# An eleventh 2 MB place for expert weights from the start, the first value projection in one stream of both weight parts, and the last tokens turned before a gather

## The chip, the cores and the metric

The kernel runs on one core of one Trainium2 chip. Its time is the device time of one execution in microseconds (us). The engines are TensorE (PE in the profile; PEld is its weight loading), VectorE (DVE), ScalarE (ACT), GpSimd (POOL) and SyncE (SP, which here only issues DMA). Each engine works through its own instructions in the order in which the program wrote them; semaphores order the engines among each other.

## The reference

One decoder layer for 256 tokens of width 1024, all in float32:

```python
proj = h @ w_in[layer]                       # 1024 -> 4360 columns
qa, ka, va, qf, kf, vf, fl, ga, gf = jnp.split(proj, split_points, axis=-1)
ya = sliding_window_sink_attention(qa, ka, va, sink) @ w_proj_swa     # 8 heads, 2 key/value heads, window 128
yf = forgetting_attention(qf, kf, vf, log_sigmoid(fl + b_forget)) @ w_proj_fox   # 8 heads
mix = sigmoid(ga) * ya + sigmoid(gf) * yf
h = layer_norm(ALPHA * h + mix @ w_out)
m = moe(h)        # softmax router, top 4 of 32 experts, clamped SwiGLU, 1024 -> 2 x 1024 -> 1024
h = layer_norm(ALPHA * h + m)
```

The 32 experts hold 8 MB of gate and up weights and 4 MB of down weights each, 384 MB in all, and every one is read once.

## The kernel before

**Two phases.** The front (to about 200 us) does the input projection, both attentions, the gated mix, the output projection, the first layer norm and the routing. Then come 32 experts, each on 64 gathered token rows, two experts to a gather (`OH`, `OH0` are the one-hot matrices; `xTe` holds the gathered rows).

**Precision in the front.** A projection is made of three passes, high by high, high by low and low by high part. `split` (L108) makes the parts of a weight group: ScalarE copies the high part (L110), VectorE subtracts it to get the low part (L111). `projT` (L312 to L314) gives transposed results, `projN` (L325 to L327) results with tokens on the partitions. The weight groups of `w_in` arrive one after the other by DMA (L218) and are split by `split_in`; `evac` copies a finished PSUM tile, alternating between ScalarE (L93) and VectorE (L95, L97). PSUM tiles of projections are named `pj` and have two buffers. Group 0 is the keys of the windowed attention, group 1 its values together with the 8 forget-gate columns (128 + 8 = 136 columns), groups 2 and 3 its queries. The order in the program is

```python
split_in(0); split_in(1); split_in(2)
projT(0, ka)
split_in(3)
projN(1, [(v[:, :, 0:128], 0, 128), (fl, 128, 136)])     # both token halves in one tile pj
...
for i in range(2, 8): split_in(i + 2); projT(i, ...)
```

**Mix and output projection.** 32 pieces of `w_proj_swa`, `w_proj_fox` and `w_out` (128 x 512 each, numbered u) are split by `split_u`, most of them into the tile `w_r` with five buffers; some go into other tiles (u = 5 to 8 and the even ones from 24). The loop at L569 uses the pieces in the order 0 to 12, 14, 13, 15, twelve matmuls each (L576 to L578), and after most of them writes a split some pieces ahead. The last pieces end in the gate products and sums on VectorE (L584, L585), the mix's high and low halves (L586 on ScalarE, L566 on VectorE) and the output projection (`out_proj`, L614).

**Layer norm and routing.** `residual`, `shift`, `normed`, `turn` (transposes at L644 and their copy), `logits` (L658), `choice`, `positions` (L675) and `gather0` (L684) run for token half 0 and then for half 1. `busy` (L102) issues filler matmuls. `scaled_out` (L824, L822) writes the gathered rows of experts 0 and 1.

**Weights of the experts.** The first 32 items of 2 MB (four of gate and up, two of down per expert) go into ten places of 16 KB per partition (`slot_tile`), which the front uses for its own data, and one further place, `extra`. `load_next` issues the next item on SyncE (L127), `refill` does so as the experts use items up. In the front, places are filled as they come free: two at the first pair of heads, then behind pieces 7, 15, 15, 15, 23, 31, then two in the routing and last `extra`, when the pool `p2` of the front is closed. `extra` is used once, for item 10. From item 32 on, the memory of the ten places becomes five places of 4 MB (`ww`), each loaded with two items in one transfer.

Of the kernel before, what the change touches and what calls it, by code (L numbers as in the profile page):

```python
# [35 lines left out]
def layer(tc, x, w_in, b_forget, sink, w_proj_swa, w_proj_fox, w_out, ln1_g, ln1_b, w_router, b_router,  # L36
# [9 lines left out]
    with ExitStack() as ctx:  # L46
# [5 lines left out]
        slots = {i: small.enter_context(tc.tile_pool(name=f"slot{i}", bufs=1, side="right")) for i in reversed(slot_of[1:] + slot_of[:1])}  # L52
# [19 lines left out]
        alpha_i = per.tile([P, P], F32, name="alpha_i")  # L72
# [69 lines left out]
        def load_next(n=1):  # L142
            for _ in range(n):
                i = nxt[0]
                kind, e, q = items[i]
                if i < SMALL:
                    r = extra.tile([P, 4096], F32, name="w") if i == 10 else slot_tile(slot_of[(i - (i > 10)) % 10])
                    where[kind, e, q] = r
                    fetch(kind, slice(e, e + 1), q, r)
                    nxt[0] += 1  # L150
                    continue
                r = big_tile()
                where[kind, e] = r
                for a in range(2):
                    where[kind, e, q + a] = r[:, 4096 * a:4096 * a + 4096]
                if i + 2 < len(items):
                    fetch(kind, slice(e, e + 1), q, r, 2, 4 if i + 8 >= len(items) else 2 if i + 26 >= len(items) else 1)
                else:
                    fetch_last(r)
                nxt[0] += 2  # L160

        def refill(n, keep=0):

            used[0] += n
            while nxt[0] < len(items):
                i = nxt[0] + (nxt[0] >= SMALL)
                if i - (11 if i < 21 else 10) >= used[0] - keep:
                    break
                if nxt[0] >= SMALL and not big:
                    if used[0] < SMALL:  # L170
                        break

                    extra_ctx.close()
                    small.close()
                    for u in reversed(range(5)):
                        big.append(ctx.enter_context(tc.tile_pool(name=f"two{u}", bufs=1, side="right")))
                    big.reverse()
                load_next()
# [18 lines left out]
        with tc.tile_pool(name="hd", bufs=1) as hd:  # L197
# [25 lines left out]
            with ExitStack() as at_ctx:  # L223
# [12 lines left out]
                dve.tensor_scalar(alpha_i, ident, ALPHA, None, op0=OP.mult)  # L236
# [45 lines left out]
                def split_in(i, parts=(0, 1)):  # L282
# [3 lines left out]
                    if i not in hls:  # L286
                        tl = slot_tile(1 + i % 3, F32R)
                        hls[i] = [tl[:, 8 * n * k:8 * n * (k + 1)].rearrange("p (c n) -> p c n", n=n) for k in (0, 1)]
                    for q in parts:
                        cs = slice(4 * q, 4 * q + 4)  # L290
                        for k, r in enumerate(raws[i]):
# [5 lines left out]
                            else:  # L297
                                split(*[a[:, cs, 128 * k:128 * k + m] for a in hls[i]], r[:, cs])
# [46 lines left out]
                projN(1, [(v[:, :, 0:128], 0, 128), (fl, 128, 136)])  # L345
# [128 lines left out]
                def split_u(u):  # L474
# [7 lines left out]
                    elif u > 23 and u % 2 == 0:  # L482
                        if u == 24:
                            more2.append(slot_tile(9, F32R))
                        w_r = more2[0][:, 512 * (u - 24):512 * (u - 22)].rearrange("p (k n) -> p k n", k=2)
                    else:
                        w_r = p2.tile([P, 2, 512], F32R, name="w_r", bufs=5)
# [5 lines left out]
                for i in range(10):  # L493
# [12 lines left out]
                    if i == 0:  # L506
# [13 lines left out]
                        load_next(2)  # L520
                    if i == 7:
# [33 lines left out]
            wb = hd.tile([P, 8, NE], F32, name="wb")  # L555
            gnat = hd.tile([P, 2, 8], F32, name="gnat")
            sums = hd.tile([P, 2, NE], F32, name="sums")
# [41 lines left out]
            mv = hd.tile([P, 2, 2], F32, name="mv")  # L599
            stt = [hd.tile([P, 2, 6], F32, name=f"stt{t}") for t in range(2)]  # L600
            rs = hd.tile([P, 2], F32, name="rs")
            nm = hd.tile([P, 2], F32, name="nm")
            OH0 = hd.tile([P, 2, 2, CAP], F32, name="OH0")
            tix = hd.tile([P, 2, 8], mybir.dt.uint32, name="tix")
            iota_e = hd.tile([P, NE], F32, name="iota_e")
            lgN = hd.tile([P, 2, NE], F32, name="lgN")
            shf = hd.tile([P, 2, NE], F32, name="shf")
# [8 lines left out]
            def residual(t, k):  # L616
# [4 lines left out]
                if k:  # L621
                    dve.bn_aggr(mv[:, t], stt[t])
                    act.activation(rs[:, t:t + 1], mv[:, t, 1:2], AF.Sqrt, bias=eps)

            def shift(t):
                dve.reciprocal(rs[:, t:t + 1], rs[:, t:t + 1])
# [42 lines left out]
            def positions(t, pause=None):  # L669
# [3 lines left out]
                if pause:  # L673
                    pause(3)
# [37 lines left out]
            for c in (4, 5):  # L712
                out_proj(c, 1, 0)
            turn(0, 0, act)
            turn(0, 1, act)
            shift(0)
# [17 lines left out]
            gather0(0, 0)  # L734
            turn(1, 1, act)
            shift(1)
            logits(1, 1)
# [5 lines left out]
            busy(idle, 2)  # L743
# [6 lines left out]
            extra_ctx = ExitStack()  # L750
            extra = extra_ctx.enter_context(tc.tile_pool(name="extra", bufs=1, side="right"))
            load_next()

        with tc.tile_pool(name="mo", bufs=1) as mo:
# [193 lines left out]

            xTs[0] = mo.tile([P, 8, 2, CAP], F32, name="xTe", bufs=2)
# [16 lines left out]
            for e in range(NE):  # L966
# [18 lines left out]
                if e == REST:  # L985
# [5 lines left out]
                    act.activation(gateT, pt[:NE], AF.Copy)  # L991
                    for t in range(2):
# [128 lines left out]
```

## Time and profile before

| | |
|---|---|
| median of 3 runs | 1119.88 us (1118.96 to 1120.91) |
| profiled execution | 1119.41 us |
| its span | 1117.2 us |
| TensorE busy | 1054.9 us (94%) |
| VectorE, ScalarE busy | 378.3 us, 211.3 us |
| mean granted TensorE clock | 0.985 |
| read from memory | 430.53 MB |

The span is the time between the first and the last instruction in the profile; the execution's own time has 2.2 us more. Matmuls are pipelined, so the busy time of TensorE counts overlapping instructions once and is not a measure of full speed. A clock of 1.00 is 2.4 GHz, 0.50 is 1.2 GHz.

### The profile page before, as it was taken

Reading aid. Unit: us, or ns where it says so; the run is one execution under the profiler, and the core shown is the slowest. Engines: PE = TensorE matmul, PEld = TensorE weight load, DVE = VectorE, ACT = ScalarE, POOL = GpSimd, SP = SyncE. Lnnn points to the kernel's source line nnn. Section 1 sums busy time; section 2 is a strip of 40 time slices with the busy share of each in tenths; the row PEclk is TensorE's granted clock in tenths of the full one; section 3 lists DMA queues with packets and bytes.
Section 4 is the critical chain, followed back from the end, with each engine's and each line's share of the span. In section 5 each row is a group of like instructions: output and inputs, shape, how many; then the busy total and the mean of one; then the engine's idle time right before and its main releaser. Section 6 shows DMA issues by size and latency. Waiting matters only on the chain. (4 is left out here: it accounts for less than half of the span.)

```text
span 1117.2 us, 13432 instructions
## 1 busy us (share of the span) xinstructions
PE 1054.9 (94%) x5677; PEld 517.1 (46%) x5677; DVE 378.3 (34%) x821; ACT 211.3 (19%) x416; POOL 4.8 (0%) x14
## 2 busy tenths in 40 slices
PE   9999999999999999999999999999998988998895
PEld 8988897533333333333333343333433333333322
DVE  5577476432222224222222222222222222222223
ACT  5466464311111110000000110011000000000011
POOL 0000000000000000000000000000000000000001
PEclk9999999999999998999999999999999999999997
DMA  9754599999999999999999999999999999999993
GB/s 274 227 195 146 140 392 354 377 426 405 429 424 429 432 431 416 430 429 430 430 430 431 429 432 431 431 431 430 429 429 431 430 429 430 426 425 428 423 419 121
DMA packets 46406, 432.48 MB, mean 387 GB/s; under 512 B 5524, under 2 KB 26020, under 8 KB 29448
## 3 DMA queue, kind: packets, MB, share of 16 engines
q1 hardware_dynamic: 46144, 431.18, 93.5%
q8 instruction: 46, 0.75, 0.3%
q10 hardware_dynamic: 200, 0.41, 0.1%
q14 instruction: 16, 0.13, 0.0%
HBM read 430.53 MB, written 1.05 MB: 386 GB/s over the span
## 5 line engine op out<-in xcount | busy, mean ns | idle before, releaser
L851 PE MATMUL G<-ww,xTe 128*64 128x512 f32 x1664 | 368.2, 597 | 19.5 <-DMA ww<-in_w_gate_up_dram 19.1
L851 PEld LDWEIGHTS G<-ww,xTe 128*64 128x64 f32 x1664 | 119.3, 138 | 264.1 <-issue 227.3
L886 PE MATMUL X<-ww,aT 128*64 128x512 f32 x864 | 191.3, 595 | 0.5 <-DVE tb L871 0.3
L858 DVE COPY G_sb<-G 128x512 f32<-128x512 f32 x32 | 33.2, 1037 | 408.0 <-PE G L851 408.0
L860 ACT ACTIVATE G_sb<-G 128x512 f32<-128x512 f32 x32 | 33.8, 1055 | 422.3 <-PE G L851 422.3
L886 PEld LDWEIGHTS X<-ww,aT 128*64 128x64 f32 x864 | 59.6, 137 | 113.4 <-issue 107.6
L851 PE MATMUL G<-w,xTe 128*64 128x512 f32 x384 | 83.5, 593 | 0.6 <-POOL nth L773 0.6
L312 PE MATMUL pj<-w 128*128 128x256 f32 x232 | 66.7, 288 | 1.3 <-ACT w L110 0.8
L314 PE MATMUL pj<-w 128*128 128x256 f32 x232 | 65.7, 283 | 0.2 <-DVE w L111 0.2
L313 PE MATMUL pj<-w 128*128 128x256 f32 x232 | 65.6, 283 | 0.0
L809 PE MATMUL X<-OH,h_perm 128*128 128x128 f32 x480 | 63.0, 288 | 1.2 <-DVE h_perm L947 0.9
L900 PE MATMUL acc<-D_sb,GT 64*128 64x512 f32 x248 | 61.6, 615 | 0.7 <-DVE D_sb L893 0.7
L809 PEld LDWEIGHTS X<-OH,h_perm 128*128 128x128 f32 x480 | 60.1, 204 | 1.8 <-PE X L839 1.2
L868 PE MATMUL X<-ident,G_sb 128*128 128x128 f32 x256 | 40.0, 280 | 20.1 <-ACT xTe L822 12.0
L873 ACT ACTIVATE sg<-tb 128x256 f32<-128x256 f32 x64 | 26.7, 416 | 148.5 <-DVE tb L872 148.5
L851 PEld LDWEIGHTS G<-w,xTe 128*64 128x64 f32 x384 | 28.3, 137 | 53.6 <-issue 52.3
L893 DVE COPY D_sb<-X 128x256 f32<-128x256 f32 x31 | 13.2, 425 | 112.0 <-ACT D_sb L892 112.0
L111 DVE TENSOR_TENSOR w<-w 128x1024 fp32r<-128x1024 f32 (+2 forms) x50 | 46.3, 965 | 13.8 <-ACT w L110 13.8
L312 PEld LDWEIGHTS pj<-w 128*128 128x128 f32 x232 | 44.3, 191 | 3.9 <-issue 2.2
L871 DVE TENSOR_TENSOR tb<-X,bT 128x512 f32<-128x512 f32 x64 | 43.7, 683 | 4.1 <-PE X L868 4.1
L314 PEld LDWEIGHTS pj<-w 128*128 128x128 f32 x232 | 44.4, 191 | 0.4 <-DVE w L111 0.4
L313 PEld LDWEIGHTS pj<-w 128*128 128x128 f32 x232 | 44.4, 191 | 0.0
(263 smaller groups left out, 866.6 us busy)
## 6 DMA issues: line engine op xcount, KB each, us to landing
ww<-in_w_gate_up_dram SPq DMA_DIRECT2D x44, 4096.0 KB, 27.2
ww<-in_w_down_dram SPq DMA_DIRECT2D x23, 4096.0 KB, 28.2
w<-in_w_gate_up_dram SPq DMA_DIRECT2D x24, 2048.0 KB, 10.0
ww<-in_w_gate_up_dram SPq DMA_DIRECT2D x12, 2048.0 KB, 38.5
w<-in_w_down_dram SPq DMA_DIRECT2D x8, 2048.0 KB, 10.7
w<-in_w_in_dram SPq DMA_DIRECT2D x14, 1024.0 KB, 5.6
ww<-in_w_down_dram SPq DMA_DIRECT2D x6, 2048.0 KB, 39.7
ww<-in_w_gate_up_dram SPq DMA_DIRECT2D x8, 1024.0 KB, 28.3
```

The lines of the kernel that those rows point to most:

```text
L111: dve.tensor_tensor(lo, src, hi.bitcast(F32), op=OP.subtract)
L312: pe.matmul(pt[:, j, :], hi[:, c, cs], xh[:, c, :], start=c == 0, stop=False)
L313: pe.matmul(pt[:, j, :], hi[:, c, cs], xl[:, c, :], start=False, stop=False)
L314: pe.matmul(pt[:, j, :], lo[:, c, cs], xh[:, c, :], start=False, stop=c == 7)
L809: pe.matmul(pt[:, c, :], h_perm[:, t, c0 + c, :], OH[:, t].rearrange("p a s -> p (a s)"), start=t == 0, stop=t == 1)
L851: pe.matmul(G[hf][64 * k:64 * k + 64, :], xT_e[:, c, :], w[:, c % 2, n0:n0 + 512], start=c == 0, stop=c == 7)
L858: dve.tensor_copy(dst, src)
L860: act.activation(dst, src, AF.Copy)
L868: pe.transpose(pt[:, c].rearrange("p k s -> p (k s)"), G_sb[:, c0 + c, :], ident)
L871: dve.tensor_tensor(tb, pt, bias[:, c0:c0 + 4, :, None].to_broadcast([P, 4, 2, CAP]), op=OP.add)
L886: pe.matmul(pt[64 * k:64 * k + 64, :], aT[:, c, :], w[:, c % 4, k * 512:(k + 1) * 512], start=c == 0, stop=c == 7)
L900: pe.matmul(acc[t][k], GT[r, t * P:(t + 1) * P], D_sb[r, :], start=first, stop=False)
```

## The change

`extra` is open from the beginning and takes its place as the third of a ring of eleven; item 2 is loaded into it in the attention (pair 3), and every later load of the front is one item further. The ring of eleven holds for all 32 small items. `w_r` has four buffers instead of five, `alpha_i` is made at expert 14, and the small tiles of the layer norm and the routing (`wb`, `gnat`, `sums`, `mv`, `stt`, `rs`, `nm`, `OH0`, `tix`, `iota_e`, `lgN`, `shf`) move from the pool `hd`, which is open all through the front, to `p2`, which opens after the attention. The order of the small places in memory is turned by one. The first gathered rows take the second buffer of `xTe`.

The first values (group 1) lay their high and low parts side by side, so that one matmul of 272 columns gives high by high and high by low; each token half has a PSUM tile of its own, and the two parts are added on the way out.

In the layer norm the square root moves from `residual` to `shift`; for the first half `shift` is written ahead of the two turns, for the second half the turn and `shift` come ahead of the first gather. The filler matmuls between the second half's choice and its positions go from 2 + 3 to 1 + 1.

```diff
-        slots = {i: ... for i in reversed(slot_of[1:] + slot_of[:1])}
+        slots = {i: ... for i in reversed(slot_of[9:] + slot_of[:9])}
+        extra = extra_ctx.enter_context(tc.tile_pool(name="extra", bufs=1, side="right"))
+        ring = [*slot_of[:2], None, *slot_of[2:]]
...
-                    r = extra.tile([P, 4096], F32, name="w") if i == 10 else slot_tile(slot_of[(i - (i > 10)) % 10])
+                    r = extra.tile([P, 4096], F32, name="w", tag="w") if i % 11 == 2 else slot_tile(ring[i % 11])
...
-                if i - (11 if i < 21 else 10) >= used[0] - keep:
+                if i - (11 if nxt[0] < SMALL else 10) >= used[0] - keep:
...
+                        if i == 1:
+                            both = tl[:, :16 * n].rearrange("p (c k n) -> p c k n", k=2, n=n)
+                            hls[i] = [both[:, :, 0], both[:, :, 1], both]
...
-                projN(1, [(v[:, :, 0:128], 0, 128), (fl, 128, 136)])
+                for t in range(2):
+                    pt = pjp.tile([P, 2, 136], F32, name="pj")
+                    ts = slice(t * P, (t + 1) * P)
+                    for c in range(8):
+                        w = hls[1][2][:, c].rearrange("p k n -> p (k n)")
+                        pe.matmul(pt.rearrange("p k n -> p (k n)"), xh[:, c, ts], w, start=c == 0, stop=False)
+                        pe.matmul(pt[:, 0], xl[:, c, ts], hls[1][0][:, c, :], start=False, stop=c == 7)
+                    vl = at.tile([P, 136], F32, name="vl")
+                    act.activation(vl, pt[:, 1], AF.Copy)
+                    dve.tensor_tensor(v[:, t, 0:128], pt[:, 0, :128], vl[:, :128], op=OP.add)
+                    dve.tensor_tensor(fl[:, t], pt[:, 0, 128:], vl[:, 128:], op=OP.add)
...
-                        w_r = p2.tile([P, 2, 512], F32R, name="w_r", bufs=5)
+                        w_r = p2.tile([P, 2, 512], F32R, name="w_r", bufs=4)
...
+                    if i == 3:
+                        load_next()
...
-                    act.activation(rs[:, t:t + 1], mv[:, t, 1:2], AF.Sqrt, bias=eps)
...
             def shift(t):
+                act.activation(rs[:, t:t + 1], mv[:, t, 1:2], AF.Sqrt, bias=eps)
...
-                    pause(3)
+                    pause(1)
...
+            shift(0)
             turn(0, 0, act)
             turn(0, 1, act)
-            shift(0)
...
             residual(1, 1)
-            gather0(0, 0)
             turn(1, 1, act)
             shift(1)
+            gather0(0, 0)
             logits(1, 1)
...
-            busy(idle, 2)
+            busy(idle, 1)
...
-            extra_ctx = ExitStack()
-            extra = extra_ctx.enter_context(tc.tile_pool(name="extra", bufs=1, side="right"))
-            load_next()
...
+            mo.tile([P, 8, 2, CAP], F32, name="xTe", bufs=2)
             xTs[0] = mo.tile([P, 8, 2, CAP], F32, name="xTe", bufs=2)
...
+                    alpha_i = mo.tile([P, P], F32, name="sg", bufs=2)
+                    dve.tensor_scalar(alpha_i, ident, ALPHA, None, op0=OP.mult)
```

## Rows read from the trace of the kernel before

**Rows 1.** The page: span, moved GB/s in 40 slices, one costly group

```profile
span 1117.2 us, 13432 instructions
...
GB/s 274 227 195 146 140 392 354 377 426 405 429 424 429 432 431 416 430 429 430 430 430 431 429 432 431 431 431 430 429 429 431 430 429 430 426 425 428 423 419 121
...
L851 PE MATMUL G<-ww,xTe 128*64 128x512 f32 x1664 | 368.2, 597 | 19.5 <-DMA ww<-in_w_gate_up_dram 19.1
```

**Rows 2.** Stretches: length, busy (instructions) of PE, PEld, DVE, ACT, POOL, clock, DMA, GB/s

```profile
100.00:125.00 25.00, 25.00 (x209) 22.29 (x208) 18.84 (x44) 16.11 (x40) 0.00 (x0) 1.00 0.27 86
200.00:205.00 5.00, 4.62 (x22) 1.96 (x24) 2.71 (x11) 3.24 (x9) 0.45 (x3) 1.00 0.58 242
...
225.00:400.00 175.00, 166.02 (x840) 66.88 (x837) 45.13 (x102) 22.87 (x44) 0.00 (x0) 1.00 1.00 425
```

**Rows 3.** Timeline of SyncE: two single loads (start, length, line, transfer)

```profile
204.07 0.33 SPq L127 DMA_DIRECT2D w<-in_w_gate_up_dram  x1
...
327.37 0.33 SPq L127 DMA_DIRECT2D ww<-in_w_gate_up_dram  x1
```

**Rows 4.** Timeline of TensorE, 12 to 30 us, first matmuls of four projections

```profile
12.16 0.23 PE L325 MATMUL pj<-w 128*128 128x136 f32 x1
...
17.48 0.33 PE L312 MATMUL pj<-w 128*128 128x256 f32 x1
...
23.32 0.39 PE L312 MATMUL pj<-w 128*128 128x256 f32 x1
...
29.80 0.36 PE L312 MATMUL pj<-w 128*128 128x256 f32 x1 [0.47 <-DVE w L97]
```

**Rows 5.** Timeline of ScalarE and VectorE, 15 to 24 us

```profile
16.09 0.36 ACT L93 ACTIVATE w<-pj 128x256 f32<-128x256 f32 x1
...
20.15 1.67 ACT L110 ACTIVATE w<-w 128x512 fp32r<-128x512 f32 x3 [1.74 <-DMA w<-in_w_in_dram]
...
20.81 1.90 DVE L111 TENSOR_TENSOR w<-w 128x512 fp32r<-128x512 f32 x3 [1.68 <-ACT w L110]
22.63 0.42 DVE L95 COPY v<-pj 128x256 f32<-128x256 f32 x1
```

**Rows 6.** TensorE's three longest waits for DMA; one stretch with its clock

```profile
842.38 8.55 PE L851 MATMUL G<-ww,xTe 128*64 128x512 f32 x32 [2.52 <-DMA ww<-in_w_gate_up_dram]
...
901.34 7.09 PE L851 MATMUL G<-ww,xTe 128*64 128x512 f32 x32 [3.26 <-DMA ww<-in_w_gate_up_dram]
...
930.91 8.66 PE L851 MATMUL G<-ww,xTe 128*64 128x512 f32 x32 [3.04 <-DMA ww<-in_w_gate_up_dram]
...
842.00:844.00 2.00, 1.62 (x4) 0.53 (x6) 0.00 (x0) 0.00 (x0) 0.00 (x0) 0.50 0.99 426
```

**Rows 7.** Timeline, 158 to 164 us: first gate product, output projection

```profile
158.02 0.68 DVE L584 TENSOR_TENSOR w<-w,G 128x512 f32<-128x512 f32 x1
...
160.75 3.25 PE L614 MATMUL acc<-w_r,w 128*128 128x512 f32 x12
```

**Rows 8.** Timeline, 191 to 215 us: routing of half 1 and first expert

```profile
191.19 1.14 PE L684 MATMUL X<-OH,h_perm 128*128 128x128 f32 x8
...
192.17 0.60 PE L644 MATMUL G<-ident,x_sb 128*128 128x128 f32 x4
...
193.52 1.08 PE L658 MATMUL acc<-wr,hT 128*128 128x32 f32 x8 [0.75 <-ACT hT L647]
...
195.77 0.38 DVE L667 TENSOR_REDUCE mask<-sel 128x32 f32<-128x128 f32 x1
...
196.74 0.31 PE L675 MATMUL acc<-mask,tri 128*128 128x32 f32 x2
...
197.75 2.02 PE L684 MATMUL X<-OH,h_perm 128*128 128x128 f32 x16 [0.17 <-DVE OH L679]
...
199.87 0.41 DVE L824 TENSOR_SCALAR xTe<-X,gcol 128x128 f32<-128x128 f32 x1 [2.27 <-PE X L684]
...
200.38 13.95 PE L851 MATMUL G<-w,xTe 128*64 128x512 f32 x64 [0.61 <-POOL nth L773]
```

More of the change, by code (lines that the diff above doesn't have):

```diff
@@ L51, in layer @@
         small = ExitStack()
-        slots = {i: small.enter_context(tc.tile_pool(name=f"slot{i}", bufs=1, side="right")) for i in reversed(slot_of[1:] + slot_of[:1])}
+        slots = {i: small.enter_context(tc.tile_pool(name=f"slot{i}", bufs=1, side="right")) for i in reversed(slot_of[9:] + slot_of[:9])}
+        extra_ctx = ExitStack()
+        extra = extra_ctx.enter_context(tc.tile_pool(name="extra", bufs=1, side="right"))
+        ring = [*slot_of[:2], None, *slot_of[2:]]
         ctx.enter_context(tc.manual_schedule())
@@ L71, in layer @@
         warm = per.tile([P, 1], F32, name="warm")
-        alpha_i = per.tile([P, P], F32, name="alpha_i")
         top = per.tile([P, 2, 8], F32, name="top")
@@ L235, in layer @@
                 dve.tensor_scalar(ident, jp, 0.0, None, op0=OP.is_equal)
-                dve.tensor_scalar(alpha_i, ident, ALPHA, None, op0=OP.mult)
                 pool.iota(iota_s, pattern=[[1, CAP]], base=1, channel_multiplier=0,
@@ L297, in split_in @@
                             else:
-                                split(*[a[:, cs, 128 * k:128 * k + m] for a in hls[i]], r[:, cs])
+                                split(*[a[:, cs, 128 * k:128 * k + m] for a in hls[i][:2]], r[:, cs])
                     if 1 in parts and i != 11:
@@ L552, in acc_tiles @@
                 return [[accp.tile([P, 512], F32, name=f"acc{t}{k}") for k in range(2)] for t in range(2)]
-            wb = hd.tile([P, 8, NE], F32, name="wb")
-            gnat = hd.tile([P, 2, 8], F32, name="gnat")
-            sums = hd.tile([P, 2, NE], F32, name="sums")
+            wb = p2.tile([P, 8, NE], F32, name="wb")
+            gnat = p2.tile([P, 2, 8], F32, name="gnat")
+            sums = p2.tile([P, 2, NE], F32, name="sums")
             lower = acc_tiles()
@@ L598, in layer @@
             r = x_sb
[L599 to L607, printed above, removed]
+            mv = p2.tile([P, 2, 2], F32, name="mv")
+            stt = [p2.tile([P, 2, 6], F32, name=f"stt{t}") for t in range(2)]
+            rs = p2.tile([P, 2], F32, name="rs")
+            nm = p2.tile([P, 2], F32, name="nm")
+            OH0 = p2.tile([P, 2, 2, CAP], F32, name="OH0")
+            tix = p2.tile([P, 2, 8], mybir.dt.uint32, name="tix")
+            iota_e = p2.tile([P, NE], F32, name="iota_e")
+            lgN = p2.tile([P, 2, NE], F32, name="lgN")
+            shf = p2.tile([P, 2, NE], F32, name="shf")
             pool.iota(iota_e, pattern=[[1, NE]], base=0, channel_multiplier=0, allow_small_or_imprecise_dtypes=True)
```

## The prediction

> **What bounds the kernel now.** I read the page first, then the busy time by stretch, then the queue of the loading engine, then the waits of TensorE. The page puts 19.1 us of TensorE's waiting at the gate and up matrices on DMA [rows 1]: late in the kernel the weights, not the matmuls, set the pace. The page's slices of 28 us say how evenly: from the ninth to the last but one they carry 405 to 432 GB/s [rows 1]. The stretches say since when: DMA is full from 225 us on, and in 200 to 205 us it was only 58% busy [rows 2]. The end is therefore "the moment the weight stream gets going" plus a fixed number of bytes plus the tail. What gets it going is TensorE: the first refill is issued at 204.07 [rows 3], when the first expert, started at 200.38 [rows 8], has used its first 2 MB place; 16 of its matmuls take half of 7.09 us [rows 6], so 203.9. All eleven places were full by then, which is what the idle DMA share says. So one microsecond in the start of the experts is one microsecond at the end, and the 200 us in front of it are a TensorE matter: from 100 to 125 us TensorE counts 25.00 of 25 us busy beside a DMA share of 0.27 [rows 2].
>
> **The eleventh place.** It moves one 2 MB load from the end of the front into the attention (behind the third pair of heads' projection). At 430 GB/s 2.1 MB are 4.9 us of DMA. It is put into a stretch where DMA is 27% busy [rows 2], and SyncE queues behind it only a 1 MB load whose data are needed two projections later: cost nothing; with that cover gone, at most the 4.9 us. Gain: before and after, eleven items are resident when the first place comes free, so the stream starts no earlier by it. What remains is that eleven, not ten, places turn over among the first 32 items. The average of 225 to 400 us lies at 425 GB/s [rows 2] against 430 in most later slices [rows 1], so at most 175 x 5/430 = 2.0 us can be won there. But at 327.37 the queue again waits for TensorE to free a pair of places [rows 3], the same pair in both versions, and by then the DMA has nearly caught up: I take 0, bounds 0 and -2.0.
>
> **First values in one stream.** Before, 48 matmuls of 136 columns run from 12.16 to 17.48, 0.111 us each; the 256-column ones that follow need 5.84/48 = 0.122 us [rows 4]. So 136 columns cost hardly less than 256, and replacing three passes of 136 by one of 272 (0.122 x 272/256 = 0.129) and one of 136 saves, for 16 pairs, 5.32 - 16 x 0.240 = 1.5 us of TensorE. The Trainium skill (TensorE: Matmul & The Clock Gate, Back-to-back issue gap) gives an isolated matmul columns/2.4 GHz + 2.5 ns, which would make three passes of 136 178 ns and the new two 175 ns, so that by it even this 1.5 us would be nothing; the row's 111 ns stands here.
>
> But the two token halves now take two PSUM tiles of "pj", which has two buffers, where both halves shared one. Follow them. The first half takes the buffer that is free and runs from 12.16 to 14.1. The second needs the buffer of the key projection, whose copy sits on ScalarE behind the splits of the third weight group and runs at 16.09 for 0.36 us [rows 5]: second half from 16.5 to 18.4. The next projection needs the first half's buffer, so its ScalarE copy and its two VectorE additions. In program order these stand behind the splits of the fourth weight group, which wait for that group's data: ScalarE is through at 20.15 + 1.67 = 21.82, VectorE at 20.81 + 1.90 = 22.71 [rows 5]. The values' copy of before started just there, at 22.63, and took 0.42 us for 128x256 [rows 5]; the additions of one half are 128x128 and 128x8, about as long together. So the projection that began at 17.48 begins at about 23.15. Before, this lateness was hidden: the copy's buffer was wanted only at 23.32 [rows 4]. From there two projections of 5.8 us each run to 34.7, against 29.80 before (which holds 0.47 us of waiting, covered now [rows 4]). The later projections keep TensorE at 25.00 of 25 us [rows 2], so nothing gives it back: **+4.9 us** (4.6 to 5.2).
>
> TensorE stands idle for 2.4 us and then for 4.7 us. Three long waits of before bear on its clock: after 2.52 and 3.04 us the granted clock was 0.50 (1.2 instead of 2.4 GHz) and the next 32 matmuls took 8.55 and 8.66 us; after 3.26 us they took 7.09 [rows 6]. The gap here is longer than all three, so I take the loss, 8.6 - 7.09 = **+1.5 us**; bounds 0 and 1.6 (one fall). The Trainium skill (the same page, HAM oscillation) lets every such wait for data cost the clock; the 3.26 us row disagrees once in three, so by the page the 1.5 us are certain, and by the rows likely.
>
> **Four instead of five split buffers.** Each split writes a buffer that its earlier user must have read. With four, the split of piece 17 (ScalarE, then VectorE), written ahead of the first products with the sigmoid gate, waits for a piece among 13 to 16 to be used; before, piece 12 sufficed. A piece is 12 matmuls, 1.4 us; the last ends where the output projection starts, 160.75 [rows 7], so the last but two (piece 14) ends at 157.95 and the last but one (piece 13) at 159.35. After 0.6 us of ScalarE and 0.65 of VectorE (thirds of the rows of three splits [rows 5]) VectorE is at 159.3 or 160.7 with what began at 158.02 [rows 7]. Queued behind it are the gate products, the mix's high halves and the output projection that waits for them: +1.3 us if the buffer that comes free first is taken, +2.7 if they go round in turn. VectorE has no pause in that chain. I take **+1.3**; for the low end 0.5, part of it hidden.
>
> **Last tokens turned first.** The four transposes (192.17) go ahead of the gather (191.19, about 1 us), and the square root behind their copy. The gather then fills the copy's time, and the second logits, at 193.52 after 0.75 us of waiting, start at 191.3 + 0.6 + 1.0 = 192.95 [rows 8]: 0.55 earlier. The choice's mask, ready at 195.77 + 0.38 = 196.15, moves with it, and the position matmul, held until 196.74 by filler matmuls, of which three go, follows the mask at once: 1.0 earlier [rows 8]. The gathered rows were scaled at 199.87, only after all 16 matmuls of 2.02 us, and the experts began at 200.38, 0.61 us after the gather [rows 8]. The scaling's target and the one-hot now lie apart, so the first half is scaled under the second: 0.6 more. **-1.6** (bounds -0.9, if that wait stays, and -1.7). The multiples of the identity made later, the moved small tiles and the square root of the first half sit beside running matmuls: 0; the DVE work at the middle expert is less than 1 us at a place where TensorE's wait for DMA has not begun, so uncovered it would cost under 1.
>
> **The sum.** 4.9 + 1.5 + 1.3 - 1.6 + 0 = +6.1. The profiled execution took 1119.41 us, 2.2 of them outside its span of 1117.2 [rows 1]; it would take 1125.5. The median lies 0.47 higher: **1126.0 us**, 0.55% slower. Own range from the bounds: 4.6 + 0 + 0.5 - 1.7 - 2.0 = +1.4 to 5.2 + 1.6 + 2.7 - 0.9 = +8.6, that is 1121.3 to 1128.5.
>
> **Rivals.** (1) The copies of the first half are not held up, or the next projection gets another buffer. Then the joined stream ends at 16.0, the two projections follow with small waits for the fourth group (VectorE through at 22.71) and the place of 29.80 is reached some 1.4 us sooner. In all -1.4 + 1.3 - 1.6 = -1.7: 1118.2 us, no change or a little faster. It decides if those copies run before 17.5. For it: ScalarE and VectorE do stand idle about 18 to 20 us. Against it: the copy of before had the same idle time in front of it, with its matmuls done at 17.6, and ran at 22.63 [rows 5]. By the skill's spacing its -1.4 would be about 0 and its time 1119.6. Chance 0.13.
> (2) The end is set by bytes alone: with the eleventh place filled early the stream runs through the start of the experts, and their start does not matter. Then one place's 4.9 us are won: 1115.0 us. For it: the full DMA from 225 us on [rows 2]. Against it: the 58% in 200 to 205 us and the refill issued at 204.07, right on TensorE's first place [rows 2, 3]. Chance 0.09.
> My forecast has 0.78, and within it the variants without the fall of the clock (1124.5) or with buffers in turn (1127.4).
>
> **Numbers.** About 0.2% (2.2 us) is what a measurement of this kernel can tell from no change: faster below 1117.6, slower above 1122.1. The forecast lies slower with 0.74 and the same with 0.04; rival 1 the same with 0.08 and faster with 0.05; rival 2 faster with 0.07 and the same with 0.02. Faster 0.12, same 0.14, slower 0.74. The range 1118.5 to 1129.0 takes in the forecast's own range and half of rival 1 and leaves out rival 2.
>
> **What would show it.** Right: TensorE idle from about 18.4 to 23.1 us with VectorE's first addition near 22.7; the granted clock at 0.5 just behind; the first expert near 206.5, the first refill 3.6 us after it; DMA engines idle some microseconds before that; from there the same pace. Wrong: a next projection near 16 to 18 us (rival 1); a first expert that is late while the last weights land early (rival 2); the output projection following its last piece without a pause (no cost of four buffers); scaled rows still waiting for all 16 gather matmuls (tail -0.9 only). If the experts start late and the end is not late, my link from start to end is wrong.

## The result and the profile after

| | before | after |
|---|---|---|
| median of 5 runs | 1119.88 us | 1126.80 us (1124.71 to 1128.36) |
| profiled execution, its span | 1119.41, 1117.2 us | 1127.54, 1125.6 us |
| first expert starts | 200.38 | 208.61 |
| from there to the end of the span | 916.8 | 917.0 |
| mean granted TensorE clock | 0.985 | 0.978 |

The ratio of the runs is 1.0059, with a 95% interval of 1.0043 to 1.0074: 0.6% slower, 6.9 us, where 6.1 us were forecast. The table says where to look: the 8.2 us of the trace are all there when the experts start. The profiled executions lie further apart (8.1 us) than the medians: that of the kernel after took 0.7 us more than its median, that of before 0.5 less.

The page of the kernel after (span, moved GB/s by slice, two costly groups), as in [rows 1]:

```profile
span 1125.6 us, 13394 instructions
...
GB/s 272 178 222 206 103 340 369 297 427 427 427 425 431 428 431 420 429 431 429 428 433 432 430 430 429 431 429 428 434 429 432 429 428 429 426 427 427 422 418 105
...
L865 PE MATMUL G<-ww,xTe 128*64 128x512 f32 x1664 | 370.7, 601 | 17.0 <-DMA ww<-in_w_gate_up_dram 16.6
...
L316 PE MATMUL pj<-w 128*128 128x256 f32 x232 | 67.6, 291 | 2.5 <-DVE fl L360 1.9
```

Late in the kernel the picture is that of before: 429 GB/s or so, TensorE waiting for weights. New is the last line: projections that wait for the forget gates' addition.

The timeline of the kernel after, 12 to 28 us, answering to [rows 4, 5] (start, length, engine and line, idle time ahead and what ended it):

```profile
12.49 0.29 PE L355 MATMUL pj<-w 128*128 128x272 f32 x1
...
16.91 0.36 ACT L95 ACTIVATE w<-pj 128x256 f32<-128x256 f32 x1
...
17.32 0.59 PE L355 MATMUL pj<-w 128*128 128x272 f32 x1 [2.82 <-ACT w L95]
...
20.08 1.67 ACT L112 ACTIVATE w<-w 128x512 fp32r<-128x512 f32 x3 [1.08 <-DMA w<-in_w_in_dram]
20.75 1.90 DVE L113 TENSOR_TENSOR w<-w 128x512 fp32r<-128x512 f32 x3 [1.02 <-ACT w L112]
...
22.56 0.28 DVE L359 TENSOR_TENSOR v<-pj,vl 128x128 f32<-128x128 f32 x1
22.76 0.15 DVE L360 TENSOR_TENSOR fl<-pj,vl 128x8 f32<-128x8 f32 x1
...
23.06 0.55 PE L316 MATMUL pj<-w 128*128 128x256 f32 x1 [1.95 <-DVE fl L360]
...
27.46 0.28 PE L318 MATMUL pj<-w 128*128 128x256 f32 x1
```

The reader is to see a queue, not a slow instruction. The second token half (17.32) waits for the key copy; the next projection (23.06) waits for the first half's additions, and these stand on VectorE behind splits that wait for the fourth group's data. The stretches of the same time (length, busy and instructions of PE, PEld, DVE, ACT, POOL, clock, DMA, GB/s) show the clock:

```profile
18.00:20.00 2.00, 2.00 (x11) 2.00 (x11) 0.69 (x1) 0.63 (x1) 0.00 (x0) 0.50 1.13 331
...
24.00:26.00 2.00, 2.00 (x12) 2.00 (x11) 1.15 (x7) 1.81 (x4) 0.00 (x0) 0.50 0.99 293
...
28.00:30.00 2.00, 2.00 (x19) 2.00 (x19) 1.81 (x2) 0.00 (x0) 0.00 (x0) 1.00 0.06 19
```

At 0.50 only 11 or 12 matmuls go into 2 us, at 1.00 it is 19. The clock had fallen already behind the first wait, so that the second half itself ran slowly, and was back at about 27.4.

The timeline further on, answering to [rows 7, 8] (first mix matmul; split of piece 17 and first gate product; output projection; last gather, scaling, first expert):

```profile
145.15 0.39 PE L593 MATMUL acc<-w,w_r 128*128 128x256 f32 x1 [1.14 <-ACT w_r L112]
...
166.22 0.63 ACT L112 ACTIVATE w_r<-w 128x512 fp32r<-128x512 f32 x1 [0.94 <-PE G L595]
...
167.49 0.68 DVE L601 TENSOR_TENSOR w<-w,G 128x512 f32<-128x512 f32 x1
...
169.61 0.73 PE L631 MATMUL acc<-w_r,w 128*128 128x512 f32 x2 [0.56 <-ACT w L603]
...
170.88 2.60 PE L631 MATMUL acc<-w_r,w 128*128 128x512 f32 x10 [0.53 <-DVE w L583]
...
205.95 2.05 PE L701 MATMUL X<-OH,h_perm 128*128 128x128 f32 x16 [0.27 <-ACT h_perm L651]
...
208.10 0.41 DVE L838 TENSOR_SCALAR xTe<-X,gcol 128x128 f32<-128x128 f32 x1 [2.39 <-PE X L701]
...
208.61 6.66 PE L865 MATMUL G<-w,xTe 128*64 128x512 f32 x30 [0.61 <-POOL nth L787]
```

The split at 166.22 waits for TensorE, with the gate product behind it; the output projection now has pauses (0.56, 0.53) where it had none [rows 7]. The scaling at 208.10 still begins after all 16 gather matmuls. And 145.15 shows what the prediction did not have: 1.14 us of waiting for a split of `w_proj_swa`. The same line of before, with the one where the third dozen of output matmuls begins (177.21 in the kernel after):

```profile
137.59 0.39 PE L576 MATMUL acc<-w,w_r 128*128 128x256 f32 x1 [0.23 <-ACT w_r L110]
...
167.75 0.50 PE L614 MATMUL acc<-w_r,w 128*128 128x512 f32 x1 [0.59 <-ACT w_r L110]
```

The stretch around the start of the experts, in the kernel after (columns as above, DMA share and GB/s last):

```profile
205.00:215.00 10.00, 9.12 (x52) 5.00 (x53) 5.03 (x18) 4.48 (x11) 0.46 (x3) 1.00 0.30 103
```

DMA is busy for 30% of these 10 us; from 208 to 212 it moves 4 GB/s. The first refill is issued at 212.30, 3.7 us after the first expert started, which is the distance of before (204.07 and 200.38 [rows 3, 8]).

### The profile page after: what moved, and what is told of

Same layout as the page of the kernel before. It is cut to its first block, busy times and chain, and to the rows that moved or that the text cites. A ratio compares the mean times of both kernels' runs of the same rounds, so it can differ in the third digit from the quotient of the medians.

```text
span 1125.6 us, 13394 instructions
## 1 busy us (share of the span) xinstructions
PE 1060.5 (94%) x5655; PEld 520.9 (46%) x5655; DVE 379.3 (34%) x824; ACT 212.3 (19%) x417; POOL 4.8 (0%) x14
## 5 line engine op out<-in xcount | busy, mean ns | idle before, releaser
L316 PE MATMUL pj<-w 128*128 128x256 f32 x232 | 67.6, 291 | 2.5 <-DVE fl L360 1.9
L318 PE MATMUL pj<-w 128*128 128x256 f32 x232 | 66.5, 287 | 0.2 <-DVE w L113 0.2
L317 PE MATMUL pj<-w 128*128 128x256 f32 x232 | 66.5, 287 | 0.0
L316 PEld LDWEIGHTS pj<-w 128*128 128x128 f32 x232 | 45.3, 195 | 5.0 <-issue 4.3
L318 PEld LDWEIGHTS pj<-w 128*128 128x128 f32 x232 | 45.4, 196 | 0.4 <-DVE w L113 0.4
L317 PEld LDWEIGHTS pj<-w 128*128 128x128 f32 x232 | 45.4, 196 | 0.0
## 6 DMA issues: line engine op xcount, KB each, us to landing
ww<-in_w_down_dram SPq DMA_DIRECT2D x23, 4096.0 KB, 27.4
```

Source lines behind the costliest of these rows:

```text
L316: pe.matmul(pt[:, j, :], hi[:, c, cs], xh[:, c, :], start=c == 0, stop=False)
L317: pe.matmul(pt[:, j, :], hi[:, c, cs], xl[:, c, :], start=False, stop=False)
L318: pe.matmul(pt[:, j, :], lo[:, c, cs], xh[:, c, :], start=False, stop=c == 7)
```

## The experiments

The theory was the prediction's: first values that hold up the next projection, and four split buffers that block a split. The runs of before beside each group had medians of 1119.74, 1119.92 and 1120.00 us.

**The stream alone.** Before, with the edits of the first values only (the shared tile of `projN(1, ...)` replaced by the block in the diff).

> The kernel before with one part of the change alone: first values in one stream, each token half in a pj tile of its own. My theory (copies of the first half queue behind the splits of the fourth weight group, TensorE idles, its clock falls): next projection begins near 23.1 instead of 17.48, granted clock 0.5 behind it, experts start 6.4 to 6.7 us later than 200.38, time 1126.3 to 1126.6. Rival (the loss of the whole change comes from the eleventh place, its memory order or the four buffers; the stream itself gains its 1.5 us): 1118.4.

1127.46 us, ratio 1.0072 [1.0058, 1.0085]. The rows:

```profile
23.31 0.36 PE L315 MATMUL pj<-w 128*128 128x256 f32 x1 [1.93 <-DVE fl L359]
...
145.01 0.38 PE L592 MATMUL acc<-w,w_r 128*128 128x256 f32 x1 [1.16 <-ACT w_r L110]
...
207.81 7.52 PE L867 MATMUL G<-w,xTe 128*64 128x512 f32 x34 [0.61 <-POOL nth L789]
```

The stream makes the experts 7.4 us late by itself. Rival 1 falls.

**All but the stream.** The changed kernel with `projN(1, ...)` put back.

> The changed kernel with the first values done as before (three passes, one tile for both halves); all else stays. My theory: the changed kernel's 1126.8 less 6.7 us, so 1120.1, that is the kernel before plus what four buffers cost (1.3 to 1.9) less what the last tokens win (1.1), within 1 us of the kernel before. Rival (eleventh place, memory order or buffers carry the loss): 1126 or above. Rival 2 of the prediction (place filled early gives the stream 4.9 us): about 1115.

1118.53 us, ratio 0.9990 [0.9981, 0.9999], first expert 201.50: 1.6 us better than expected. A gain is missing from the sum.

**Four buffers alone.**

```diff
-                        w_r = p2.tile([P, 2, 512], F32R, name="w_r", bufs=5)
+                        w_r = p2.tile([P, 2, 512], F32R, name="w_r", bufs=4)
```

> The kernel before with four instead of five split buffers and nothing else. My theory: the split of piece 17 waits for a later piece, VectorE reaches the gate products 1.3 us late, output projection starts 1.3 us after its last piece of before (160.75), experts 1.3 to 1.9 us later: 1121.2 to 1121.8. Rival (hidden by VectorE's and ScalarE's spare time): 1119.9, experts at 200.4.

1122.02 us, ratio 1.0021 [1.0011, 1.0030], +2.3 us by the medians. In the trace the first mix matmul is at 138.22 and the output projection runs so:

```profile
162.46 0.73 PE L614 MATMUL acc<-w_r,w 128*128 128x512 f32 x2 [0.64 <-ACT w L586]
163.73 2.60 PE L614 MATMUL acc<-w_r,w 128*128 128x512 f32 x10 [0.54 <-DVE w L566]
...
170.07 0.51 PE L614 MATMUL acc<-w_r,w 128*128 128x512 f32 x1 [0.59 <-ACT w_r L110]
```

From 138.22 to 170.07 are 31.85 us, against 30.16 before: 1.7 us. Two pauses, not one: the blocked split delays the gate products, and the mix's low half after them.

**Fillers in the gaps.** The changed kernel with filler matmuls behind each half:

```diff
                         pe.matmul(pt[:, 0], xl[:, c, ts], hls[1][0][:, c, :], start=False, stop=c == 7)
+                    busy(idle, 16 if t else 9)
```

> The changed kernel with filler matmuls in TensorE's two idle gaps of the first values (9 calls behind the first half, 16 behind the second). My theory: granted clock stays 1.00 from 12 to 30 us, the next projection still begins near 23.1 (the copies are as late as before), and the time falls by the 1.5 us of slow matmuls: 1125.3. If instead the wait itself were the whole cost: clock back at 1.00 and still 1126.8.

1124.85 us, ratio 1.0044 [1.0030, 1.0057], 1.95 us less than the changed kernel. The stretch that ran at 0.50, and the first mix matmul on the timeline:

```profile
24.00:26.00 2.00, 2.00 (x19) 2.00 (x19) 1.51 (x9) 1.25 (x2) 0.00 (x0) 1.00 0.96 279
```

```profile
143.06 0.39 PE L594 MATMUL acc<-w,w_r 128*128 128x256 f32 x1 [0.41 <-ACT w_r L112]
```

Each call gives two matmuls in the trace, 18 and 32 in all. The clock was 1.00 from 16 us on; expected was from 12 us, but in this execution it had fallen to 0.50 at 12 to 14 us, behind a wait of 1.48 us ahead of the fillers. The gain is two things. At the first scores of the attention (58.34 against 59.69) it is 1.35 us: the projection behind the values takes 5.82 us (23.63 to 29.45) instead of 7.74 (23.06 to 30.80), 1.9 less, and the fillers put its start off by 0.6. Another 0.7 are there at the first mix matmul, whose wait fell from 1.14 to 0.41 us. Why fillers at 20 us shorten a wait at 143 us is taken up below.

**Other buffers for the halves.**

```diff
-                    pt = pjp.tile([P, 2, 136], F32, name="pj")
+                    pt = scp.tile([P, 384], F32, name="sc")[:, :272].rearrange("p (k n) -> p k n", k=2)
```

> The changed kernel, with the two token halves of the first values in PSUM tiles of the attention's pool (named sc) instead of the projections' two buffers pj. My theory says that the joined stream loses only by its buffers: the second half then follows the first at about 14 us, the next projection needs no value copy and starts near 16, the gap of 4.7 us and the fall of the clock go, and the time is that of the changed kernel without the stream (1118.5 us) less up to 1.4 us for the shorter stream: 1117.1 to 1118.5 us. Rival: the idle time comes from the split of the next weight group, not from the buffers; then TensorE stands still until about 22 us as before and the time stays near 1126.8 us.

1122.05 us, ratio 1.0020 [1.0010, 1.0031]: a miss of 4 us. The second half followed without a pause, but the stall moved:

```profile
31.68 0.55 PE L316 MATMUL pj<-w 128*128 128x256 f32 x1 [3.30 <-DVE w L99]
...
141.87 0.39 PE L593 MATMUL acc<-w,w_r 128*128 128x256 f32 x1 [1.34 <-ACT w_r L112]
```

The third projection behind the values waits for a query copy that stands behind later splits; the 1.5 us of TensorE that the stream saves are idle time here. Behind this wait the clock was 0.50 (32 to 34 us) and the projection took 7.2 us. In the kernel with the later split (below), which is the same up to here, the wait was 2.16 us, the clock stayed at 1.00, and the first scores came at 54.52 instead of 56.23. The first mix matmul again waits over 1 us.

**Stream in those buffers and last tokens, five split buffers, no eleventh place.** The same line, with the first values and the last tokens of the diff, on the kernel before.

> The kernel before with the joined stream in sc tiles and the edits of the last tokens (turned before the gather, fewer filler matmuls), without the eleventh place and with five split buffers. My theory: stream up to -1.4 us, last tokens -1.1 us as measured in the changed kernel, together 1117.2 to 1118.6 us. Rival: without the eleventh place an earlier start of the experts only lets them wait longer for DMA, and the time stays at 1119.7 us.

1121.91 us, ratio 1.0020 [1.0008, 1.0031]. The experts start at 200.14, hardly earlier than before, since the first mix matmul waits 1.26 us. From there the profiled execution takes 2.7 us longer than that of before; half of it stands in one stretch, where the clock was 0.88 and DMA moved 315 GB/s, 1.4 us short of the 433 that a sister kernel (own memory, below) moved at a clock of 1.00. A fall of the clock in the first experts holds up the places and so the stream. The other half was not traced to a cause. The stretch, and the timeline of the scaling:

```profile
222.00:227.00 5.00, 5.00 (x24) 1.75 (x22) 2.81 (x12) 0.00 (x0) 0.00 (x0) 0.88 0.87 315
```

```profile
199.63 0.41 DVE L840 TENSOR_SCALAR xTe<-X,gcol 128x128 f32<-128x128 f32 x1 [2.40 <-PE X L700]
...
200.14 1.08 PE L867 MATMUL G<-w,xTe 128*64 128x512 f32 x4 [0.61 <-POOL nth L789]
```

**A later split.** The kernel with the other buffers, with pieces 17 and 18 split one piece later:

```diff
-                if n < 5 or n > 8:
+                if n < 5 or 8 < n < 12 or n > 13:
                     split_u(n + 9 if n < 5 else n + 5)
+                if n == 13:
+                    split_u(17)
+                    split_u(18)
```

> As the changed kernel with sc tiles, and the splits of pieces 17 and 18 written one piece later each (with the loop's thirteenth piece both), so that with four split buffers none waits on ScalarE for a piece still to be used. My theory says that the four buffers cost 1.3 to 2.3 us by these blocked splits: the time falls by 1 to 2 us against the kernel with sc tiles alone, to about 1116 us. Rival: the split of piece 17 is needed where it stands, or the wait only moves to the piece's use; then no change against it.

1122.60 us, ratio 1.0019 [1.0007, 1.0031]: no gain in the time, although the mix takes 31.1 instead of 32.1 us. Inconclusive on this base; repeated below on a quieter one.

**Place and buffers.** Before with the eleventh place, its ring, the moved tiles and four buffers.

> The kernel before with the eleventh place, its ring, the moved small tiles and four split buffers, but with the first values and the last tokens as before. If the place wins nothing, as predicted, this is the cost of the four buffers alone, 1122.0 us. If the early eleventh place wins the 1.2 us that the DMA shortfall suggests, up to 2.0 us, it comes to 1120.0 to 1120.8 us; its distance to the changed kernel without the stream (1118.5 us) is then the last tokens' gain.

1120.28 us, ratio 1.0008 [0.9999, 1.0018]: 1.7 us under what the four buffers alone take, 1.75 above the kernel without the stream. So the place (with its ring and the moved tiles) wins something, and the last tokens too. Where the place wins: in the kernel before, with ten places turning over, DMA had one dip in the first experts; in the kernel after, 8.2 us later, it has none.

```profile
265.00:275.00 10.00, 10.00 (x50) 3.55 (x51) 4.60 (x12) 1.22 (x3) 0.00 (x0) 1.00 0.93 374
```

```profile
273.00:283.00 10.00, 9.93 (x48) 3.63 (x50) 4.80 (x13) 1.23 (x4) 0.00 (x0) 1.00 1.01 428
```

(The first row is before, the second after.) The 56 GB/s missing over 10 us of 430 are 1.3 us. The dip belongs to the kernels without the place: in the 20 us that begin 60 us after the first expert, DMA moved 387 to 405 GB/s in all six profiles without it and 420 to 428 in all eight with it.

**No stream and the later split.** The kernel without the stream, with the edit of the later split.

> The changed kernel without the joined stream (first values as before), and with the splits of pieces 17 and 18 written one piece later each. In the kernel with sc tiles this late split removed the wait of 0.56 and 0.53 us at the output projection and left 0.5 us more waiting a few pieces on; from the first mix matmul to the third dozen of output matmuls it took 31.1 us instead of 32.1. Expected: 1.0 us under the changed kernel without the stream (1118.5 us), 1117.5 us, and faster than the kernel before (1119.8 us). Rival: the clock falls of the first experts decide more than 1 us, and no difference is seen.

1117.50 us, ratio 0.9976 [0.9965, 0.9987]: as expected, and faster than both kernels.

```profile
137.41 0.39 PE L580 MATMUL acc<-w,w_r 128*128 128x256 f32 x1
...
168.52 0.49 PE L621 MATMUL acc<-w_r,w 128*128 128x512 f32 x1 [1.10 <-ACT w_r L112]
...
199.92 13.95 PE L855 MATMUL G<-w,xTe 128*64 128x512 f32 x64 [0.61 <-POOL nth L777]
```

31.11 us between the first two rows, against 32.07 without the later split (138.01 to 170.08) and 30.16 before. The two pauses at the output projection are gone, at the price of 0.5 us more waiting at 168.52: the blocked split was what made them.

**Fillers put back.** The kernel with stream and last tokens, with fillers where TensorE stood idle:

```diff
                     split_in(i + 2)
+                    if i == 4:
+                        busy(scp.tile([P, 384], F32, name="sc")[:, :P], 16)
```

> The kernel before with the joined stream in sc tiles and the edits of the last tokens, plus 16 filler matmuls ahead of the third projection behind the values, where TensorE stood idle for 2.1 us anyway. Theory: the load of the windowed attention's output weights lands 1.0 us late because a 16 KB instruction fetch falls into its transfer, and the fetch stands there because TensorE's program is shorter by 16 matmuls ahead of it. With 16 matmuls put back, the fetch falls ahead of that load as in the kernel before, the wait at the first mix matmul is 0.2 us instead of 1.26, and the first expert starts 1 us earlier, at about 199.1 us. Rival: the late landing comes from something else in the joined stream; the wait stays at 1.1 to 1.3 us and the first expert at 200.1 us or later.

1119.98 us, ratio 0.9997 [0.9988, 1.0006]. The 16 calls give 32 matmuls in the trace, twice as many as the stream took out. The first mix matmul no longer waits for its split, as expected; the first expert did not come earlier (201.14), since the front was 2.6 us behind that without fillers at the first scores (55.30 against 52.69); the fillers, 3.5 us long where 2.1 were idle, are 1.4 of that, and 0.7 were there when the values began. The DMA view over the transfer of `w_proj_swa` (instruction fetches with their MB; size and median time to landing), of the kernel after and then of this one, with this one's first mix matmul:

```profile
q8 instruction: 1, 0.02, 0.6%
...
w<-in_w_proj_swa_dram SPq DMA_DIRECT2D x2, 1024.0 KB, 11.3
```

```profile
w<-in_w_proj_swa_dram SPq DMA_DIRECT2D x2, 1024.0 KB, 10.0
```

```profile
139.45 0.33 PE L594 MATMUL acc<-w,w_r 128*128 128x256 f32 x1
...
140.12 0.39 PE L596 MATMUL acc<-w,w_r 128*128 128x256 f32 x1 [0.22 <-DVE w_r L111]
```

Over the first 10 us from the issue, a fetch of 16 KB lies in the transfer in all seven kernels that have the stream and no fillers, and their landings take 10.9 to 11.5 us. In before and the four without the stream none does, nor in the two with fillers, and there it takes 10.0 to 10.6. The fetch begins 0.3 us ahead of the load's issue in the kernel before (122.97), 4.8 us behind it in the kernel after (134.73), and 2.4 us ahead of it here (123.10). The trace does not name the engine that fetches; that it is TensorE is inferred, since of the programs ahead of the load this experiment lengthens TensorE's alone.

**One line moved.** The changed kernel with the fourth group's splits written behind the values:

```diff
-                split_in(3)
                 for t in range(2):
...
+                split_in(3)
```

> The changed kernel with one line moved: the splits of the fourth weight group are written behind the value projection instead of ahead of it, the two pj buffers stay. My theory: the second token half still waits for the key copy behind the third group's splits, until 16.5 us or with a fall of the clock 17.3, but the first half's copies then run ahead of the fourth group's splits, at about 17 us, and the next projection starts right behind the second half, at 18.4 to 20.8 us instead of 23.1. The first expert starts 2.3 to 4.7 us earlier than in the changed kernel (208.6), and the time is 1122 to 1124.5 us. Rival: the next projection waits for the second half's buffer too, or the later splits come too late for the projection after it, and the time stays at 1126.8 us.

1123.00 us, ratio 1.0015 [1.0004, 1.0025]; the runs lie in two groups, 1118.5 to 1120.6 and 1122.8 to 1124.1, and the profiled one is of the lower.

```profile
16.19 0.39 PE L354 MATMUL pj<-w 128*128 128x272 f32 x1 [2.15 <-ACT w L95]
...
203.47 11.81 PE L865 MATMUL G<-w,xTe 128*64 128x512 f32 x54 [0.61 <-POOL nth L787]
```

The second wait of the kernel after is gone and the experts start 5.1 us earlier: the order of the queue made that wait, and 3.8 us of the medians with it. The first wait, for the key copy, is still there, as forecast, and the clock was 0.50 behind it (18 to 20 us).

**Own memory for the gathered rows.** The kernel with stream and last tokens, with

```diff
-                    xTs[g] = mo.tile([P, 8, 2, CAP], F32, name="xTe", bufs=2)
+                    xTs[g] = per.tile([P, 8, 2, CAP], F32, name="xTe", bufs=2)
```

and the same for `xTs[0]`.

> The kernel before with the joined stream in sc tiles and the edits of the last tokens, with the gathered rows (xTe) moved from the experts' pool to the pool that is open from the start. Theory: the first half of the gathered rows is scaled only after all 16 gather matmuls because its memory is taken over from the front's pool, whose last use is the last gather matmul. With memory of its own it is scaled under the second half of the gather, and the first expert starts 0.4 to 0.6 us earlier behind the gather's begin (2.1 instead of 2.66 us). Rival: the scaling waits for the matmuls themselves, and the distance stays 2.66 us. The time is within 1 us of the kernel without this edit (1121.9 us).

1121.62 us, ratio 1.0013 [1.0004, 1.0023]. The timeline, and the stretch in which the kernel without this edit had slowed down:

```profile
197.55 2.05 PE L700 MATMUL X<-OH,h_perm 128*128 128x128 f32 x16 [0.28 <-ACT h_perm L650]
198.75 0.41 DVE L840 TENSOR_SCALAR xTe<-X,gcol 128x128 f32<-128x128 f32 x1 [1.46 <-PE X L700]
...
199.53 0.65 PE L867 MATMUL G<-w,xTe 128*64 128x512 f32 x2
```

```profile
222.00:227.00 5.00, 5.00 (x26) 1.72 (x24) 2.18 (x9) 0.00 (x0) 0.00 (x0) 1.00 1.02 433
```

The scaling begins under the gather, and the first expert 1.98 us behind its begin instead of 2.66. The wait belonged to the memory that the experts' pool takes over from the front, not to the matmuls.

## Why the prediction was right, point by point

The time was 1126.8 where 1126.0 was forecast, and the likeliest case was the one that came. But three terms of its sum were mis-sized and two were missing. In the trace these errors add up, and the experts start at 208.61 where the forecast had them near 206.5. That the median came within 0.8 us is partly luck: the five runs of the kernel after spread over 3.7 us.

- **Bound: the start of the experts sets the end.** Held: the start is 8.2 us later, the first refill follows it by 3.7 us as before, with DMA idle ahead of it, and from the start on the two profiled executions take 917.0 and 916.8 us. Rival 2 (bytes alone) falls.
- **First values, +4.9, and the clock, +1.5.** The mechanism held to the instruction: next projection at 23.06 (23.15 forecast), first addition at 22.56 (22.7). With the stream alone the first scores are 6.5 us late (59.52 against 53.00), for 6.4 forecast; without the stream they lie at 53.0 to 53.7 in five profiles. The clock fell one wait earlier than I had it, behind 2.82 us rather than the second gap; what the fall cost the second half vanished in the gap that followed. The slow matmuls behind that gap cost 1.9 us rather than 1.5. By the Trainium skill (TensorE: Matmul & The Clock Gate, HAM oscillation) a long wait for data costs the clock each time; the rows agree for 3.29 us (stream alone) and 3.30 us (other buffers) and disagree for 3.26 us late in the kernel before [rows 6] and 3.41 us late with four buffers alone. Shorter waits went either way: behind 1.48 us (fillers), 2.15 us (moved line) and 2.82 us the clock was 0.50, behind 2.12, 2.16 and 2.17 us in three other kernels it stayed at 1.00.
- **Missing term: the instruction fetch, +0.9.** With 16 matmuls taken out of TensorE's program a later fetch, which lay 0.3 us ahead of the load of `w_proj_swa`, fell into it, and the mix waited 1.14 instead of 0.23 us. The Trainium skill (Runtime: NRT & Kernel Launch, Instruction fetch mechanics) says that programs are refilled in 16 KiB blocks and that crossing one is mostly hidden. The block's size is what the rows show (0.02 MB); here a fetch put off a load of weights by about 1 us, and the mix with it.
- **Four buffers, +1.3.** Right in place and size for the kernel after: the split of piece 17 blocks the gate products, and from the first mix matmul to the third dozen of output matmuls (145.15 to 177.21) it takes 1.9 us longer than before, 0.6 of it ahead of the pauses. Alone the buffers cost 1.7 us in the trace, 2.3 by the medians.
- **Missing term: a slower mix, +0.6.** From the first to the last of the mix's 192 matmuls it is 23.63 us in the kernel after, 23.04 before; 23.62 to 23.64 in all eight profiles with the eleventh place and its moved tiles, 22.99 to 23.33 in the six without. Most of it is the spacing. In the kernel before, a piece of twelve matmuls takes 1.40 us, and 1.44 for pieces 5 to 8, whose split parts lie in other tiles; with the place the others take 1.44 too, with four buffers alone they stay at 1.40. That points to where the tiles lie in memory and not to the number of buffers; it was not tried. The other 0.13 us are a pause in the fourteenth piece, which four buffers alone have too (0.29).
- **Last tokens, -1.6.** Too much: from the second half's first transposes (188.31 before, 197.62 after) to the first expert it took 12.07 us before and 10.99 after, -1.1. The 0.6 for the scaling under the gather failed; that was named as what would show it, with -0.9. I had the target of the scaling free; it waited for the pool's memory. With memory of their own the rows win 0.7 (1.98 instead of 2.66 us behind the gather's begin).
- **Eleventh place, 0.** Wrong, within its bounds of 0 to -2.0. I argued that DMA would have caught up by 327 us anyway; it does not: 130 us after the first expert 104.0 MB had been moved in the kernel before and 104.4 in the kernel after, 0.8 us of DMA. From the first expert to the last group of gate matmuls that waits for a load, the profiled executions with the place take 877.1 to 877.3 us (no stream, with and without the later split; other buffers; the moved line), before and three others without it 878.0 to 878.2 (four buffers, fillers later, own memory): -0.9. Left out are executions with a further fall of the clock (877.7 to 879.8 with the place, 881.8 without), and the stream alone, which took 1.7 us longer than before, unexplained. Over all profiles the medians are 877.5 with the place and 878.2 without. By the medians of the run times of the buffers with and without the place it is 1.9.

In the kernel after this last gain does not show (878.26 us), because the clock fell once more late: 835 us after the first expert it was still 1.2 us ahead of the kernel before, as the one without the stream was by 1.1. The same expert of the kernel after, and of the one without the stream:

```profile
1052.20 10.09 PE L865 MATMUL G<-ww,xTe 128*64 128x512 f32 x32 [2.79 <-DMA ww<-in_w_gate_up_dram]
```

```profile
1043.67 3.65 PE L852 MATMUL G<-ww,xTe 128*64 128x512 f32 x16 [1.26 <-DMA ww<-in_w_gate_up_dram]
1048.58 3.65 PE L852 MATMUL G<-ww,xTe 128*64 128x512 f32 x16 [1.26 <-DMA ww<-in_w_gate_up_dram]
```

From 1043.67 on, the 32 matmuls with the wait between them take 8.56 us; behind one wait of 2.79 the clock fell and the same matmuls took 10.09. Such falls move single executions by 1 to 2 us. That they make the two groups of runs of the moved line is likely, not shown: the timed runs have no trace, but their mean granted clock is 0.982 to 0.984 in the lower group and 0.977 to 0.981 in the upper. What makes a given execution take the one wait or the two stays open.

**The sum as measured**, in the trace up to the first expert: 6.7 (first scores 59.69 against 53.00) + 0.9 + 1.3 + 0.6 - 1.1 = 8.4, against 8.2 read directly; behind it nothing net.

## What to carry to other kernels

Before giving a result two PSUM tiles instead of one, list what is queued ahead of the copies that free them: an engine that looks idle in the profile may be waiting, in order, for someone else's data. A saving on an engine is worth what the next wait leaves of it: the joined stream saved 1.5 us of TensorE and, with its stall moved to a later projection, 0.3 at the first scores (52.69, stream and last tokens, against 53.00). And a pool that opens over another's memory waits for that memory's last reader, whatever the data say.

## What the hardware showed unexpectedly

- A change of 16 matmuls at 12 us put off the landing of a load at 130 us by about 1 us (11.3 against 10.4 us with the stream alone), by one 16 KB instruction fetch; a kernel can pay for where its code is cut.
- A fall of TensorE's clock in the first experts cost DMA 1.4 us in one stretch (315 instead of 433 GB/s over 5 us), at a time when DMA was the bound: it delays the freeing of places.
- Twelve matmuls of 256 columns took 1.40 us with the split weights in one set of tiles and 1.44 in another, in the same kernel and at the same granted clock.
